# Two one-hot operands change places, gathered rows begin 14 steps later, and the query weights' low parts alternate between two engines

## The chip, the cores and the metric

One core of a Trainium2 chip runs the kernel. The metric is the device time of the program in microseconds, as the median of the runs. A second number, the span, is the time from the first to the last instruction of one profiled execution.

## The reference, cut to what matters

The reference is one encoder layer for 512 tokens of width 2048: a projection, gated linear attention and windowed attention, an output projection, and then a channel mixer with 128 x 128 = 16384 one-neuron experts. Each token has 8 heads; a head picks 16 experts by two lists of 128 keys. So a token has 128 slots, each with an expert (i, j) and a gate. The change lies in the mixer:

```python
qry = (xt @ w_query).reshape(T, PEER_HEADS, 2, PEER_QDIM // 2)
sc = jnp.einsum('thcd,hckd->thck', qry.astype(f32), sub_keys.astype(f32))
top_s, top_i = lax.top_k(sc, PEER_TOPK)
...
best_s, best_pos = lax.top_k(cand_s, PEER_TOPK)
idx = jnp.take_along_axis(cand_i, best_pos, axis=-1)
gates = jax.nn.softmax(best_s, axis=-1)
...
    u = expert_down[ib]
    act = jax.nn.gelu(jnp.einsum('tkd,td->tk', u, xb).astype(f32))
    vv = expert_up[ib]
    return jnp.einsum('tk,tkd->td', (gb * act).astype(vv.dtype), vv)
```

## The kernel before

The instructions of each engine stand in the order in which the program emits them; each engine takes its own in that order. Float32 products with weights are made as three fp32r matmuls (`mm3`): the high part of both operands, high by low, and low by high. A weight tensor comes through the class `Stream`: `load` fetches it, ScalarE casts the high part (`high`, L71), and `low` (L79) subtracts it from the raw weights on the engine that `add` was given, VectorE where nothing is said. `next` hands out a piece and prepares the one after it.

Three stages matter here.

**The query stage** (L972 on, 900 to 1170 us) runs over 8 heads. A head needs four weight pieces of 128x1024 (`wl4x` is a low part), eight (a, c) pairs of matmuls each. Between the pieces it emits the top-k work of the heads before: `pieces` runs `side` and `pairs` on VectorE, and `decode`, whose one-hot sums `oh` (L876 to L882) run on GpSimd. The four low parts of a head are made on GpSimd, VectorE, GpSimd and GpSimd.

**The gate stage** (L1127 on, 1186 to 1456 us) has 88 steps of four tokens. 352 of the 512 tokens are "dense": their activations are made for all experts and weighted by a 128 x 128 gate matrix. The matrix of one token is a product over its 128 slots: the one-hot of j (stationary) by the one-hot of i times the gate (moving). `one_hots` makes both, two steps ahead: the comparison `e` and the weighting `w` on VectorE, the copy `wj` on ScalarE, which also turns it so that the 128 keys of one token are contiguous. `w` keeps the four tokens innermost, so `w[0][:, :, u]` takes every fourth float. ScalarE copies the result to `gs`, and every eighth step stores it to `gt_d`. In between stand 246 `filler` pieces, three fp32r matmuls of 352 columns each, of the dense down product.

**The dense stage** (L1294 on, from 1472 us) has 16 rounds of 8 x 128 experts. A round's last 16 pieces multiply by the up weights (`wl2x`), 24 matmuls each; before them, from the third round on, come two half pieces for each down product. In the first two rounds the activations made before (`pre`) are weighted by the gates and split into `ah` and `al` by the class `Weighted`, partly read back from `pre_d`. After each piece `after` counts a step, and from that count starts the gathered rows: the other 160 tokens get their experts' rows by indirect DMA on GpSimd's queue (`fetch_rows`, two ahead, L1179), 1 MB each, and one VectorE instruction of 2048 columns for each row (L1193 for the down rows, L1208 for the up rows). `END` is 322, the number of rows and closing pieces, and there are 472 steps.

Of the kernel before, what the change touches and what calls it, by code (L numbers as in the profile page):

```python
# [16 lines left out]
OP = mybir.AluOpType  # L17
# [13 lines left out]
NK = 128  # L31
# [4 lines left out]
class Stream:  # L36
# [53 lines left out]
    def next(self, ahead=None):  # L90
        n = self.at
        self.halve(n + 1 + min(self.ahead if ahead is None else ahead, n))
        self.at += 1
        r = self.split[n]
        self.split[n] = None
        return r
# [3 lines left out]
def layer(ctx, tc, A, out_t, out_g, out_b):  # L100
    nc = tc.nc
    ctx.enter_context(tc.manual_schedule())

    def pool(stack, name, bufs=1, **kw):
        if kw.get("space") is not DRAM:
            kw["reuse_waits"] = "tile"
        return stack.enter_context(tc.tile_pool(name=name, bufs=bufs, **kw))

    def copy(out, in_, scale=None):
        if scale is None:  # L110
            nc.scalar.copy(out, in_)
        else:
            nc.scalar.activation(out, in_, AF.Copy, scale=scale)
# [69 lines left out]
    ws = Stream(nc, wp, "w", 2, 3, 1)  # L183
# [10 lines left out]
            ws.add(A["wout"][k, :, a:a + 4, :])  # L194
    for k in range(8):
        for a in range(0, NT, 8):
            ws.add(A["wq"][k, :, a:a + 8, :], 2, (nc.gpsimd, nc.gpsimd if a else None))

    ps = pool(front, "ps", space=PSUM)

    def pj():
        return ps.tile([128, 512], F32, name="pj", tag="pj", bufs=5)

    def pa():
        return ps.tile([128, 512], F32, name="pa", tag="pa", bufs=3)
# [4 lines left out]
    with ExitStack() as st:  # L210
# [6 lines left out]
        with ExitStack() as s2:  # L217
            ld = pool(s2, "ld", side="right")
            xt = []
            for q in range(8):  # L220
                t = ld.tile([128, 2, S], F32, name=f"xt{q}")
                for a in range(0, 2, 2 if q else 1):
                    w = 2 if q else 1
# [24 lines left out]
            for q in range(8):  # L248
                if q:
                    x_split(q, (0, 1))  # L250
                for a in range(2):
# [4 lines left out]
                    dt, k = 2 * q + a, a if q else 0  # L256
# [8 lines left out]
            for dt in range(NT):  # L265
                mm3(o_gd[:48, :], wh[:, dt, :], wl[:, dt, :], xh[:, dt, :], xl[:, dt, :], dt == 0, dt == NT - 1)
                if dt == 3:
                    b = pa()
                    for t in range(NB):
                        nc.tensor.matmul(b[:, t:t + 1], sq[:, t * 128:(t + 1) * 128], ones[:, 0:1],  # L270
                                         start=True, stop=True)
# [20 lines left out]
        with ExitStack() as s2:  # L292
# [22 lines left out]
            gd = gl.tile([48, S], F32, name="gd")  # L315
# [163 lines left out]
        with ExitStack() as s2:  # L479
# [134 lines left out]
            for g in range(3):  # L614
                e = clock[0] - 1
# [117 lines left out]
    gd = sp.tile([128, DENSE], F32, name="gd")  # L733
# [8 lines left out]
    E = 8  # L742
    EARLY, INSIDE = 3, 15
    PRE = EARLY + INSIDE + 2
# [13 lines left out]
    with ExitStack() as st:  # L758
# [133 lines left out]
        def pieces(n):  # L892
            for _ in range(min(n, len(todo))):
                todo.pop(0)()
# [10 lines left out]
        def flush():  # L905
            if late:
                late.pop().finish()
# [64 lines left out]
        for h in range(8):  # L972
            o = [pj() if h else pa() for _ in range(2)]
            for q in range(4):
                w = ws.next()
# [58 lines left out]
        def pre_store():  # L1034
            e = len(pre)
            kept = e < E
            t = prep.tile([128, DENSE], F32, name=f"pre{e}" if kept else "spill", bufs=1 if kept else 2)
            nc.vector.tensor_tensor(t, banks.pop(0), rb2[:, :DENSE], op=OP.mult)
            if not kept:
                nc.scalar.dma_start(pre_d[e], t)  # L1040
            pre.append(t)
# [8 lines left out]
        def turned_part(sel, first, n):  # L1050
            b = pa()
            for k in range(128 // n):
                rows = slice(n * k, n * k + n)
                for c in range(3):
                    nc.tensor.matmul(b[rows, c * n:(c + 1) * n], sel[rows, c, :], ident[rows, rows], start=True, stop=True)
            copy(ij[:, :, first:first + n], b[:, :2 * n].rearrange("p (c t) -> p c t", t=n))
            copy(gd[:, first:first + n], b[:, 2 * n:3 * n])

        def acts(n, *a):
            for _ in range(n):  # L1060
                yield from pre_act(*a)
# [24 lines left out]
    with ExitStack() as st:  # L1086
        gp = pool(st, "gp")
        io4 = gp.tile([128, 128, 4], BF16, name="io4")
        for k in range(4):
            if k == 0:  # L1090
                nc.gpsimd.tensor_copy(qs, ident[:, 0:NB2])
            else:
                nc.gpsimd.tensor_tensor(qs, qs, ident[:, NB2 * k:NB2 * k + NB2], op=OP.add)
        nc.vector.tensor_copy(io4, io.unsqueeze(2).to_broadcast([128, 128, 4]))

        def fill():
            yield from tail
            yield from acts(INSIDE, pa, True)

        filler, given, inside = fill(), 0, 16 * (EARLY + INSIDE) - HEAD  # L1100

        def gathered_slots():

            for b, sel in enumerate((sel_a, sel_b)):
                nc.vector.scalar_tensor_tensor(ga[b], sel[:, 0, :], 128.0, sel[:, 1, :], op0=OP.mult, op1=OP.add)
                nc.vector.tensor_copy(idx[b], ga[b])
                nc.scalar.copy(gate[b], sel[:, 2, :])

        es = {}
        STEPS = DENSE // 4  # L1110

        def one_hots(n):

            if n >= STEPS:
                return
            ts = slice(4 * n, 4 * n + 4)
            e = gp.tile([128, 2, 128, 4], BF16, name="e", bufs=3)
            nc.vector.tensor_tensor(e, ij[:, :, ts].unsqueeze(2).to_broadcast([128, 2, 128, 4]),
                                    io4.unsqueeze(1).to_broadcast([128, 2, 128, 4]), op=OP.is_equal)
            w = gp.tile([128, 128, 4], F32, name="w", bufs=3), gp.tile([128, 4, 128], F32, name="wj", bufs=3)  # L1120
            nc.vector.tensor_tensor(w[0], e[:, 0], gd[:, ts].unsqueeze(1).to_broadcast([128, 128, 4]), op=OP.mult)
            nc.scalar.copy(w[1], e[:, 1].rearrange("p k t -> p t k"))
            es[n] = w

        for k in range(2):
            one_hots(k)
        for n in range(STEPS):  # L1127
            if n % 8 == 0:
                gs = gp.tile([128, 128, 32], F32, name="gs", bufs=2)
            one_hots(n + 2)  # L1130
            if n % 4 == 1 and n < 64:
                pieces(1)
            if n in (20, 36, 52, 68):
                flush()
            if n == 38:
                turned_part(sel_h, 256, 64)
            if n == 40:
                turned_part(sel_q, 320, 32)
            while given < (n + 8) * inside // (STEPS + 8):
                next(filler)  # L1140
                given += 1
            w = es.pop(n)
            b = pj().rearrange("p (t i) -> p t i", i=128)
            for u in range(4):
                nc.tensor.matmul(b[:, u, :], w[1][:, u, :], w[0][:, :, u], start=True, stop=True)  # L1145
            copy(gs[:, :, n % 8 * 4:n % 8 * 4 + 4], b.rearrange("p t i -> p i t"))
            if n % 8 == 7:
                nc.scalar.dma_start(gt_d[n // 8].rearrange("j a x -> j (a x)"), gs.rearrange("p i t -> p (i t)"))
            if n == 70:
                gathered_slots()  # L1150
            if banks and (given + HEAD) % 16 >= 5:
                pre_store()
        for _ in filler:
            pass
        assert not todo and not late
# [26 lines left out]
    def weights_of_slots():  # L1182

        for b in range(2):
            nc.scalar.activation(ga[b], ga[b], AF.Gelu_apprx_tanh, scale=rg[:, b:b + 1])
            nc.vector.tensor_tensor(ga[b], ga[b], gate[b], op=OP.mult)
# [56 lines left out]

    pipe = []
    steps, gathered = [0], [0]
    total = 32 * (NK // E) - 2 * PRE - 12
    END = len(events)
    wait_slots = [0]

    def advance():  # L1250
        for w in pipe:
            w.step()
        while pipe and pipe[0].done == 3:
            pipe.pop(0)

    def after():

        advance()
        steps[0] += 1
        if wait_slots[0]:  # L1260
            wait_slots[0] -= 1
            if wait_slots[0] == 0:
                weights_of_slots()
            return
        while gathered[0] < min(END, steps[0] * END // total):
            gather(gathered[0])
            gathered[0] += 1
            if gathered[0] == TURN:
                wait_slots[0] = 2
                return  # L1270
# [23 lines left out]
    for sb in range(NK // E):  # L1294
        for e in range(len(av), sb * E + E):
            bank = pa()[:, :DENSE]
            for q in range(2):
                act_half(bank, q)
                after()
            av.append(Weighted(e, bank=bank))  # L1300
            pipe.append(av[-1])
        for dc in range(4):
# [8 lines left out]
            for q in range(4):  # L1311
                hi, lo = ws.next()
                for c in range(4):
                    cs = slice(c * 128, (c + 1) * 128)
                    for b in range(2):
                        w = av[sb * E + 2 * q + b]
# [86 lines left out]
```

## Time and profile before

| what | us |
|---|---|
| runs | 3346.09, 3346.30, 3348.21 |
| median | 3346.3 |
| the profiled execution | 3346.58 |
| its span | 3344.7 |
| TensorE busy | 3291.1 (98%) |
| VectorE busy | 2361.9 (71%) |
| ScalarE busy | 1183.0 (35%) |
| GpSimd busy | 917.5 (27%) |

PE is TensorE's matmuls, PEld its weight loads, DVE VectorE, ACT ScalarE, POOL GpSimd, SP the queue for plain DMAs. Matmuls overlap in the records: the distance from one start to the next tells their cost, not the length of one. An fp32 matmul leaves two records, an fp32r matmul one. Every time below is counted from the start of the span.

### The profile page before, as it was taken

To read this page: it belongs to the slowest core of one execution; us is meant where nothing else is said; L and a number is where in the kernel's file an instruction comes from. 1 tells how busy PE (TensorE), PEld (TensorE's weight loads), DVE (VectorE), ACT (ScalarE), POOL (GpSimd) and SP (SyncE) were. 2 spreads that over 40 slices of the span, in tenths; PEclk is the share of its full clock that TensorE was granted. 3 is DMA by queue.
4 is the path that set the end of the run, shared out by engine and by line. 5 is a ranking of instruction groups with operands and counts; after the bars stand their busy time and mean duration, and the time that the engine had idled before them with its cause. 6 is when DMAs were issued, how large, how long until landed. Compare 5 with 4: busy or idle time off the path is not lost.

```text
span 3344.7 us, 47641 instructions
## 1 busy us (share of the span) xinstructions
PE 3291.1 (98%) x19090; PEld 3085.0 (92%) x19090; DVE 2361.9 (71%) x3754; ACT 1183.0 (35%) x1892; POOL 917.5 (27%) x714
## 2 busy tenths in 40 slices
PE   8999999999999999998999999999999999999999
PEld 6777888888889999998999999999999999999999
DVE  5545444454456678757888888888888888888885
ACT  4334444443322245442332332332332332333332
POOL 3112020201235544322232232322232332232330
PEclk9999999999999999999999999999999999999999
DMA  4222222224322233468989898898988888988885
GB/s 148 89 91 88 76 77 84 92 101 143 117 84 72 78 126 149 156 252 337 336 327 339 324 347 331 333 350 322 338 323 327 329 338 336 334 335 330 330 347 206
DMA packets 156078, 772.94 MB, mean 231 GB/s; under 512 B 13136, under 2 KB 63632, under 8 KB 69520
## 3 DMA queue, kind: packets, MB, share of 16 engines
q1 hardware_dynamic: 99168, 388.59, 33.2%
q0 software_dynamic: 48768, 348.73, 26.4%
q10 hardware_dynamic: 7920, 32.57, 2.5%
q8 instruction: 150, 2.46, 0.3%
q14 instruction: 72, 0.59, 0.1%
HBM read 733.07 MB, written 36.77 MB: 230 GB/s over the span
## 4 chain that ended last, share of the span: by engine, by line
PE 88%; DVE 5%; DMA 2%; POOL 2%; ACT 2%; issue 1%; SPq 0%; ACTq 0%; POOLq 0%; DVEq 0%
PE pj L122 17%; PE pj L120 17%; PE pj L121 17%; PE pa L122 9%; PE pa L120 9%; PE pa L121 9%; PE pj L1145 5%; PE pa L603 1%; PE pa L544 1%; DVE wl2x L79 1%; DMA wr4x<-in_upT_dram 1%; PE pa L564 1%; DVE row L1193 1%; ACT wh2x L71 1%; POOL oh L880 0%
## 5 line engine op out<-in xcount | busy, mean ns | idle before, releaser
L79 DVE TENSOR_TENSOR wl2x<-wr4x,wh2x 128x1024 fp32r<-128x1024 f32 x382 | 467.9, 1232 | 338.7 <-ACT wh2x L71 336.0
L120 PE MATMUL pj<-ah,wh2x 128*128 128x352 f32 x2048 | 663.6, 324 | 9.3 <-ACT wh2x L71 8.9
L122 PE MATMUL pj<-ah,wl2x 128*128 128x352 f32 x2048 | 666.3, 325 | 6.3 <-DVE wl2x L79 6.3
L120 PE MATMUL pa<-yh,wh8x 128*128 128x352 f32 x2000 | 668.9, 334 | 0.0
L121 PE MATMUL pj<-al,wh2x 128*128 128x352 f32 x2048 | 661.7, 323 | 1.3 <-DVE al L1242 1.2
L122 PE MATMUL pa<-yh,wl8x 128*128 128x352 f32 x2000 | 651.5, 326 | 2.5 <-DVE wl8x L79 1.4
L121 PE MATMUL pa<-yl,wh8x 128*128 128x352 f32 x2000 | 645.3, 323 | 0.0
L71 ACT CAST wh2x<-wr4x 128x1024 fp32r<-128x1024 f32 x382 | 397.6, 1048 | 678.4 <-DMA wr4x<-in_upT_dram 337.1
L1179 POOL DMA_INDIRECT row<-in_up_dram,idx x160 | 275.8, 1724 | 610.7 <-DVE xn L1208 466.4
L1179 POOL DMA_INDIRECT row<-in_down_dram,idx x160 | 261.0, 1631 | 647.4 <-DVE ga L1193 639.5
L122 PEld LDWEIGHTS pj<-ah,wl2x 128*128 128x128 f32 x2048 | 386.5, 189 | 13.0 <-DVE wl2x L79 10.3
L120 PEld LDWEIGHTS pj<-ah,wh2x 128*128 128x128 f32 x2048 | 386.3, 189 | 12.1 <-ACT wh2x L71 10.5
L121 PEld LDWEIGHTS pj<-al,wh2x 128*128 128x128 f32 x2048 | 387.5, 189 | 2.3 <-DVE al L1242 2.1
L120 PEld LDWEIGHTS pa<-yh,wh8x 128*128 128x128 f32 x2000 | 377.5, 189 | 1.7
L121 PEld LDWEIGHTS pa<-yl,wh8x 128*128 128x128 f32 x2000 | 377.3, 189 | 1.6
L122 PEld LDWEIGHTS pa<-yh,wl8x 128*128 128x128 f32 x2000 | 374.2, 187 | 4.0 <-DVE wl8x L79 1.9
L79 DVE TENSOR_TENSOR wl8x<-wr16x,wh8x 128x1024 fp32r<-128x1024 f32 x220 | 268.3, 1222 | 106.6 <-ACT wh8x L71 106.3
L71 ACT CAST wh8x<-wr16x 128x1024 fp32r<-128x1024 f32 x256 | 266.8, 1046 | 183.5 <-DMA wr16x<-in_downT_dram 123.4
L1208 DVE SCALAR_TENSOR_TENSOR xn<-row,ga,xn 128x2048 f32<-128x2048 f32 x127 | 297.9, 2345 | 0.0
L1193 DVE CUSTOM_DVE_ANT_0 row<-row,xn 128x2048 f32<-128x2048 f32 x128 | 292.4, 2284 | 0.0
L120 PE MATMUL pj<-wh2x,xh 128*128 128x512 f32 x704 | 284.7, 404 | 0.0
L121 PE MATMUL pj<-wl2x,xh 128*128 128x512 f32 x704 | 275.4, 391 | 1.2 <-DVE wl2x L79 1.2
(330 smaller groups left out, 4959.7 us busy)
## 6 DMA issues: line engine op xcount, KB each, us to landing
wr16x<-in_downT_dram SPq DMA_DIRECT2D x128, 1024.0 KB, 7.1
wr4x<-in_upT_dram SPq DMA_DIRECT2D x128, 1024.0 KB, 7.1
wr4x<-in_win_dram SPq DMA_DIRECT2D x47, 1024.0 KB, 4.9
gt_d<-gs ACTq DMA_DIRECT2D x11, 2048.0 KB, 6.5
g<-gt_d SPq DMA_DIRECT2D x30, 704.0 KB, 8.5
wr4x<-in_wout_dram SPq DMA_DIRECT2D x16, 1024.0 KB, 5.0
wr8x<-in_wq_dram SPq DMA_DIRECT2D x16, 1024.0 KB, 5.0
xt<-in_xT_dram POOLq DMA_DIRECT2D x4, 1024.0 KB, 6.5
```

The lines of the kernel that those rows point to most:

```text
L71: self.nc.scalar.copy(hi, t)
L79: self.lo_engine[n].tensor_tensor(lo, t, hi.bitcast(F32), op=OP.subtract)
L120: nc.tensor.matmul(out, sh, mh, start=first, stop=False)
L121: nc.tensor.matmul(out, sh, ml, start=False, stop=False)
L122: nc.tensor.matmul(out, sl, mh, start=False, stop=last)
L544: nc.tensor.matmul(sc[u], qt[:, h, t * 128:(t + 1) * 128], kt[:, h, :], start=True, stop=True)
L564: nc.tensor.transpose(tp[:, kb * 128:(kb + 1) * 128], prs[u][:, kb * 128:(kb + 1) * 128], ident)
L603: nc.tensor.matmul(oo, vv[:, kb, h * 128:(h + 1) * 128], pt[u][:, kb, :], start=kb == 0, stop=kb == NB - 1)
L1145: nc.tensor.matmul(b[:, u, :], w[1][:, u, :], w[0][:, :, u], start=True, stop=True)
L1179: nc.gpsimd.indirect_dma_start(out=t, out_offset=None, in_=A["up" if up else "down"], in_offset=bass.IndirectOffsetOnAxis(ap=idx[b][:, k:k ...
L1193: nc.vector.tensor_tensor_reduce(t, t, x, 1.0, 0.0, OP.mult, OP.add, g[:, k:k + 1])
L1208: nc.vector.scalar_tensor_tensor(x, t, g[:, k:k + 1], x, op0=OP.mult, op1=OP.add)
```

## The change

Three edits. First, `add` for the query weights gives GpSimd the first piece of each load and VectorE the second. Second, in the gate stage the gate is multiplied onto the one-hot of j, which becomes the stationary operand and is read in steps of four floats; the plain one-hot of i is turned by ScalarE and streamed contiguously. The product is the same. Third, no row is started in the first 14 steps, and the count of steps over which the rows are spread is 448 and no longer 460.

```diff
-            ws.add(A["wq"][k, :, a:a + 8, :], 2, (nc.gpsimd, nc.gpsimd if a else None))
+            ws.add(A["wq"][k, :, a:a + 8, :], 2, (nc.gpsimd,))
...
-            nc.vector.tensor_tensor(w[0], e[:, 0], gd[:, ts].unsqueeze(1).to_broadcast([128, 128, 4]), op=OP.mult)
-            nc.scalar.copy(w[1], e[:, 1].rearrange("p k t -> p t k"))
+            nc.vector.tensor_tensor(w[0], e[:, 1], gd[:, ts].unsqueeze(1).to_broadcast([128, 128, 4]), op=OP.mult)
+            nc.scalar.copy(w[1], e[:, 0].rearrange("p k t -> p t k"))
...
-                nc.tensor.matmul(b[:, u, :], w[1][:, u, :], w[0][:, :, u], start=True, stop=True)
+                nc.tensor.matmul(b[:, u, :], w[0][:, :, u], w[1][:, u, :], start=True, stop=True)
...
-    total = 32 * (NK // E) - 2 * PRE - 12
+    total = 32 * (NK // E) - 2 * PRE - 24
...
-        while gathered[0] < min(END, steps[0] * END // total):
+        while gathered[0] < min(END, max(0, steps[0] - 14) * END // total):
```

On GpSimd, in the query stage, this is the end of the top-k chain of one head and the low parts behind it:

```order
 L880 TENSOR_TENSOR oh<-oh 128x128
 L882 TENSOR_TENSOR sel_d<-oh 128x2x2x16
-L79 TENSOR_TENSOR wl4x_7509<-wr8x_7176,wh4x_7507 128x1024
 L79 TENSOR_TENSOR wl4x_7576<-wr8x_7301,wh4x_7574 128x1024
 L79 TENSOR_TENSOR wl4x_7737<-wr8x_7511,wh4x_7735 128x1024
```

The low part of the head's fourth piece leaves the place behind `sel_d`. On VectorE it comes in at this place of the same head, behind the comparison `eqa`:

```order
 L869 TENSOR_SCALAR smk<-bv 128x1 x2
 L873 TENSOR_TENSOR eqa<-pf,io_7039 128x1024
+L79 TENSOR_TENSOR wl4x_7509<-wr8x_7176,wh4x_7507 128x1024
 L784 TENSOR_TENSOR xb<-pa,g2b 128x512
 L928 TENSOR_TENSOR qT<-pj,rb_6105 128x512 x2
```

It is the same in the other heads. On VectorE at the start of the dense stage, where the last of the first eight `al` is made and the first two groups of the first round end, there stood before (ISA is the row instruction and the read of its sum):

```order
L1236 TENSOR_TENSOR pre_10975<-pre_10975,g 128x352
L1193 ISA row,ga_9855<-row,xb 128x2048
L1193 ISA ga_9855 128x1
L79 TENSOR_TENSOR wl2x_12738<-wr4x_12563,wh2x_12736 128x1024
L1242 TENSOR_TENSOR al<-pre_10975,ah 128x352
L1193 ISA row,ga_9855<-row,xb 128x2048
L1193 ISA ga_9855 128x1
L79 TENSOR_TENSOR wl2x_12773<-wr4x_12646,wh2x_12771 128x1024
L1321 TENSOR_TENSOR x_12484<-x_12484,pj 128x352 x4
```

The same place now:

```order
L1236 TENSOR_TENSOR pre_10975<-pre_10975,g 128x352
L79 TENSOR_TENSOR wl2x_12735<-wr4x_12563,wh2x_12733 128x1024
L1242 TENSOR_TENSOR al<-pre_10975,ah 128x352
L79 TENSOR_TENSOR wl2x_12767<-wr4x_12646,wh2x_12765 128x1024
L1321 TENSOR_TENSOR x_12484<-x_12484,pj 128x352 x4
```

The rows between the low parts are gone here; the first one now stands at the sixteenth step, at the end of the first round.

## Rows read from the trace of the kernel before

**Rows 1.** The chain that ended last: shares of the span by engine.
```profile
PE 88%; DVE 5%; DMA 2%; POOL 2%; ACT 2%; issue 1%; SPq 0%; ACTq 0%; POOLq 0%; DVEq 0%
```
**Rows 2.** Stretches: us, busy PE, PEld, DVE, ACT, POOL; PEclk, DMA share, GB/s.
```profile
900.00:1170.00 270.00, 255.21 (x1796) 246.92 (x1796) 154.13 (x775) 73.30 (x163) 126.67 (x98) 0.97 0.23 77
...
1186.00:1390.00 204.00, 204.00 (x1077) 193.12 (x1076) 174.82 (x385) 102.56 (x179) 82.87 (x46) 1.00 0.38 144
1390.00:1456.00 66.00, 66.00 (x341) 62.72 (x340) 36.25 (x50) 31.16 (x52) 11.99 (x5) 1.00 0.40 148
...
1456.00:1540.00 84.00, 73.97 (x424) 70.63 (x423) 52.21 (x65) 25.88 (x37) 19.04 (x13) 0.94 0.88 333
1540.00:1640.00 100.00, 93.63 (x565) 90.23 (x565) 85.30 (x105) 34.85 (x49) 28.60 (x17) 1.00 0.91 335
...
1640.00:2340.00 700.00, 700.00 (x4320) 698.96 (x4319) 591.65 (x656) 221.45 (x265) 203.69 (x125) 1.00 0.89 335
```
**Rows 3.** Waits, 900 to 1190 us: who for whom, us, times, longest.
```profile
PE pj L122 <- POOL wl4x L79: 14.6, 6, 3.0
...
PEld pj L122 <- POOL wl4x L79: 16.4, 6, 3.3
```
**Rows 4.** Timeline around the first such wait: start, length, instruction, [idle before <-releaser].
```profile
934.29 0.69 DVE L873 TENSOR_TENSOR eqa<-pf,io 128x1024 bf16<-128x1024 bf16 x1
...
939.79 0.69 DVE L784 TENSOR_TENSOR xb<-pa,g2b 128x512 f32<-128x512 f32 x1 [4.82 <-ACT xr L783]
...
934.95 1.03 ACT L71 CAST wh4x<-wr8x 128x1024 fp32r<-128x1024 f32 x1
...
939.70 0.30 POOL L882 TENSOR_TENSOR sel_d<-oh 128x64 f32<-128x64 bf16 x1
...
939.96 4.70 POOL L79 TENSOR_TENSOR wl4x<-wr8x,wh4x 128x1024 fp32r<-128x1024 f32 x2
...
942.38 0.43 PE L122 MATMUL pj<-yh,wl4x 128*128 128x352 f32 x1 [2.90 <-POOL wl4x L79]
```
**Rows 5.** Groups of instructions of VectorE: low parts, row instructions.
```profile
L79 DVE TENSOR_TENSOR wl8x<-wr16x,wh8x 128x1024 fp32r<-128x1024 f32 x220 | 268.3, 1222 | 106.6 <-ACT wh8x L71 106.3
...
L1193 DVE CUSTOM_DVE_ANT_0 row<-row,xn 128x2048 f32<-128x2048 f32 x128 | 292.4, 2284 | 0.0
```
**Rows 6.** Busy time by stretch, right after two of the waits.
```profile
942.00:947.00 5.00, 4.62 (x23) 4.63 (x23) 0.00 (x0) 0.15 (x1) 2.66 (x2) 0.66 0.73 231
...
1012.00:1018.00 6.00, 5.35 (x21) 5.35 (x22) 0.00 (x0) 0.37 (x1) 2.92 (x2) 0.50 0.53 175
```
**Rows 7.** Chain and timeline: start, length, records of fp32 matmuls and of weight loads.
```profile
1314.88 0.16 PE pa L121
...
1316.18 1.81 PE pj L1145 x8
...
370.30 1.79 PE pa L603 x16
...
899.55 0.97 PEld L795 LDWEIGHTS pa<-ones,sq 128*128 128x128 f32 x8
```
**Rows 8.** Instructions of tile e, VectorE: ns minimum/median/maximum.
```profile
L1118 DVE TENSOR_TENSOR e<-ij,io x88: 669/685/2883, 1174.6 to 1445.4; 128x1024 bf16<-128x1024 bf16 x88
L1121 DVE TENSOR_TENSOR w<-e,gd x88: 691/693/2880, 1176.4 to 1446.1; 128x512 f32<-128x512 bf16 x88
```
**Rows 9.** The first rounds of the dense stage: waits, chain, and stretches.
```profile
PE pj L120 <- ACT wh2x L71: 7.9, 3, 6.0
PE pj L122 <- DVE wl2x L79: 5.4, 8, 1.3
...
1503.64 11.88 DMA wr4x<-in_upT_dram
...
1506.00:1520.00 14.00, 7.65 (x38) 6.91 (x38) 3.30 (x6) 3.04 (x3) 0.00 (x0) 0.76 0.85 350
...
1550.00:1560.00 10.00, 6.68 (x37) 5.52 (x36) 9.86 (x16) 3.75 (x7) 3.22 (x2) 1.00 0.76 259
```

## The prediction

> **What bounds the kernel now.** I read the chain of waits first. It runs through TensorE for 88% of the span [rows 1]. So work on another engine counts only where TensorE waits for it, and a change in TensorE's own instructions counts in full, until another engine becomes later. Next I read the busy time by stretch, and it names three places [rows 2]. In the query stage (900 to 1170 us) TensorE is busy 255.21 of 270 us, at a mean granted clock of 0.97. In the gate stage (1186 to 1456 us) it is never idle. In the first two rounds of the dense stage (1456 to 1640 us) it is idle 10.0 + 6.4 us. From 1640 to 2340 us it is busy without a gap although VectorE is busy 591.65 of 700 us. The diff has one edit for each of the three places.
>
> **Part 1, the low parts of the query weights.** In each of the 8 rounds over the heads, one of the three 128x1024 subtractions on GpSimd moves to VectorE. The waits tell why it matters: TensorE's matmuls wait for GpSimd's `wl4x` six times, 14.6 us in all, and the weight loads 16.4 us [rows 3]. One of them in full: the high part is ready at 934.95 + 1.03 = 935.98 us, but GpSimd first finishes the `oh` chain of the top-k, whose last piece is the `sel_d` at 939.70 us, and starts `wl4x` at 939.96; the matmul at 942.38 us has waited 2.90 us. VectorE, behind its `eqa` at 934.29 us, is idle 4.82 us until 939.79 [rows 4]. In the new order the subtraction stands exactly there, between `eqa` and `xb`. At 1.22 us (the mean of VectorE's `wl8x` row of the same size [rows 5]) it would be done near 937.2 us, before TensorE asks at about 939.3. On GpSimd the next round's `wl4x` moves up by 2.4 us; TensorE needs that one a whole granule later.
>
> A wait costs more than its length. [...] The first stretch loses (1 - 0.66) x 5 = 1.7 us, the third (1 - 0.50) x 6 less what of it lies in the wait itself, 2.7 us. Four of the six waits are near 3 us and are followed by this (3 x 1.7 + 2.7 = 7.8 us); after the two of 1.4 us the clock stays at 1.0.
> The sum: 16.4 (wait up to the weight load) + 7.8 = 24.2 us; I take 24. Lower bound: the two short waits stand where VectorE is itself busy with the top-k, and some others could be only shortened: 15. Upper bound 25. The 8 x 1.22 = 10 us added to VectorE cost nothing: it is busy 154.13 of 270 us there [rows 2]. But VectorE runs in order, so the top-k pieces behind the moved subtraction wait with it for the high part; what waits for those is GpSimd's `oh` and, much later, the selections. That is slack of several us each round.
>
> **Part 2, the one-hots change roles.** A step makes four fp32 128x128 matmuls, two records each. In the gate stage eight records take 1.81 us, 0.226 each; where the moving operand is contiguous (L603, same shape and type) sixteen take 1.79 us, 0.112 each [rows 7]. The moving operand `w` is read here in steps of four floats, so the step doubles the streaming. A weight load of 128 contiguous columns costs 0.111 us: eight loads whose matmuls have a single column take 0.97 us, which is seven distances and one last load of 0.192 [rows 7]. At L603 load and stream therefore tie at 0.11 and overlap; at L1145 the stream of 0.226 hides the load. The swap gives the stream 0.112. It gives the load the step of four floats, and no row of the trace has a load with a step. Bounds:
> - The load is as fast as a contiguous one: a step takes 8 x 0.112 = 0.90 instead of 1.81 us, 88 x 0.91 = 80 us less on TensorE.
> - The load doubles as the stream does, to 0.222, still under the matmul before it: 0.06 (the first load against a 0.16 us matmul) + 7 x 0.222 + 0.112 = 1.73 us, 88 x 0.08 = 7 us less.
> - The load doubles and does not overlap: 8 x (0.222 + 0.112) = 2.67 us, 88 x 0.86 = 76 us more.
> I take the second, since the nearest row is the same tile read with the same step by the same engine. [...]
>
> In the first case VectorE caps the gain. From 1186 to 1390 us (66 steps) it is busy 174.82 of 204 us [rows 2], and TensorE would want only 204 - 66 x 0.91 = 144; so at most 29 us can go there. From 1390 to 1456 (22 steps) VectorE needs 36.25 us only, and 20 us go in full: 49 us. Less if VectorE's stretched instructions (`e` has a median of 0.685 and a maximum of 2.883 us, `w` 0.693 and 2.880 [rows 8]) are those that meet GpSimd's work: 66 x 1.38 = 91 us of them unstretched + 82.87 us of GpSimd + some 20 us of top-k that doesn't fall under it = 194 us; then 10 + 20 = 30 us. I take 40.
>
> **Part 3, the rows begin 14 steps later.** Before, 16 x 322 // 460 = 11 gathered rows are worked off in the 16 steps of the first round; now 2 x 322 // 448 = 1. That takes 10 x 2.28 us [rows 5] of VectorE and 10 MB of row loads out of the round in which the queue is fullest. The largest wait there is 6.0 us [rows 9]: the up weights issued at 1503.64 us land after 11.88 us, with the DMA engines 0.85 busy. TensorE is busy 7.65 of 14 us in that stretch, at a granted clock of 0.76: 6.3 us idle, and of the (1 - 0.76) x 14 = 3.4 us about half while it works, together 8.0. Eight waits for VectorE's low parts, `wl2x`, make another 5.4 us, the longest 1.3 us. They come thickest from 1550 to 1560 us: there TensorE is idle 3.3 us, with VectorE busy 9.86 of 10 us [rows 9]. A low part that stands behind a row of 2.28 us loses up to that; with the rows gone I count 4 of the 5.4 us, since the waits after 1560 us lie in the round that keeps its rows. So 12 us are in reach. Other loads stay (the stored activations, x1, gates), and the new first rows still meet the last `pre` and `al` pieces: I take 10. On the other side the rows run at 322/448 = 0.719 a step for 0.700; that is 0.019 x 2.3 = 0.04 us in a step of 3.9 us, 1.1% on a VectorE that is 85% busy without stopping TensorE [rows 2]. Priced at 0, up to 5 us if it makes new waits. The last row falls on step 462 of 472, ten steps (39 us) before the end, so the tail is unmoved. Net 10, from 12 gained to 3 lost.
>
> **The sum.** 24 + 7 + 10 = 41 us off the profiled execution's 3346.6 us (span 3344.7, median 3346.3, so the same within 0.01%): **3306 us**, own range 3297 to 3324.
>
> **The rivals.**
> - *The load with a step costs nothing.* For it: a load takes 0.111 us for 128 columns where the fp32r stream takes 0.16 for 352 [rows 7], so loading is the slower reader and may have time to spare for each element. Against: the fp32 stream reads at that same pace and was slowed. It gives 24 + 40 + 10 = 74: 3273 us (3256 to 3290), with VectorE the bound of the gate stage. [...]
> - *The load with a step holds up the stream (slower).* Place: L1145, 704 records. If such a load isn't hidden under the matmul before it, the record is 0.334 instead of 0.226 us: 76 - 34 = 42 us more, 3389 us. It turns slower above a record of 0.226 + 34/704 = 0.274 us. Against: in all other rows loads are hidden.
> - *The waits come back elsewhere.* VectorE, late with the top-k, delays the moved subtractions, and the denser rows give back what the first round gains: only part 2's 7 us stay, 3340 us, at the edge of what can be told from no change (0.2% is 7 us, about the measurement's limit). Against: VectorE's idle 4.82 us at the very place.
>
> **How the numbers follow.** Chances: forecast 0.50, free load 0.36, held-up stream 0.07, waits come back 0.07. The time is the forecast's, 3306. The range takes the forecast's own range and the free load's: 3255 to 3324. Both are faster by over 0.2%: 0.86; same 0.07; slower 0.07.
>
> **What would show it.** In the changed profile: no TensorE wait for GpSimd's `wl4x`, and a granted clock of 1.0 in the query stage, 24 us shorter. Eight L1145 records in about 1.73 us (forecast), 0.90 with gaps that end on VectorE's `w` (free load), 2.67 (held up); weight loads of L1145 recorded near 0.30 us instead of 0.19 would mean the doubled load. No row before the sixteenth step, the 6.0 us wait gone. The forecast is wrong if the gate stage changes by more than 10 us either way.

## The result and the profile after

| kernel | runs | median, us (lowest to highest) | ratio, 95% interval |
|---|---|---|---|
| before | 4 | 3347.26 (3346.09 to 3350.04) | 1 |
| after | 4 | 3316.95 (3313.98 to 3324.67) | 0.9912 [0.9893, 0.9931] |

The change takes 30 us off, 0.9%. 3306 was forecast, 41 us off. The profiled execution of after took 3315.02 us, with a span of 3312.9. TensorE's share of the chain of waits is 89%, GpSimd's 0% where it was 2% [rows 1]:

```profile
PE 89%; DVE 5%; DMA 3%; ACT 2%; issue 1%; POOL 0%; ACTq 0%; DVEq 0%; POOLq 0%
```

**The query stage.** Busy time by stretch in after: TensorE is busy 267.22 of 270 us at a granted clock of 1.00, where it was 255.21 at 0.97 [rows 2]. The two stretches behind the old waits, 0.66 and 0.50 [rows 6], are at 1.00:

```profile
900.00:1170.00 270.00, 267.22 (x1909) 259.54 (x1910) 173.65 (x811) 82.25 (x178) 128.25 (x101) 1.00 0.27 89
...
942.00:947.00 5.00, 5.00 (x39) 5.00 (x38) 2.49 (x3) 0.00 (x0) 1.18 (x1) 1.00 0.20 76
1012.00:1018.00 6.00, 6.00 (x46) 5.55 (x46) 1.83 (x10) 2.95 (x5) 0.28 (x1) 1.00 0.28 107
```

All of TensorE's waits in after from 900 to 1190 us (for whom, us, times, longest). Those for GpSimd's `wl4x` [rows 3] are gone, none has come in their place (the two for `wl8x` stood there before with the same numbers):

```profile
PE pj L122 <- POOL wl8x L79: 1.3, 1, 1.3
PE pa L122 <- POOL wl8x L79: 1.1, 1, 1.1
PE pa L178 <- DVE dg L177: 0.2, 1, 0.2
```

The timeline of after at the place of [rows 4], VectorE and then GpSimd (start, length, instruction, idle before):

```profile
933.79 0.69 DVE L873 TENSOR_TENSOR eqa<-pf,io 128x1024 bf16<-128x1024 bf16 x1
935.50 2.21 DVE L79 TENSOR_TENSOR wl4x<-wr8x,wh4x 128x1024 fp32r<-128x1024 f32 x1 [1.03 <-ACT wh4x L71]
939.30 0.69 DVE L784 TENSOR_TENSOR xb<-pa,g2b 128x512 f32<-128x512 f32 x1 [1.58 <-ACT xr L783]
...
934.62 2.02 POOL L876 TENSOR_TENSOR oh<-eqa,tf 128x1024 bf16<-128x1024 bf16 x1 [4.16 <-DVE eqa L873]
936.71 3.27 POOL L880 TENSOR_TENSOR oh<-oh 128x512 bf16<-128x512 bf16 x3
```

The subtraction stands where the order put it, in what was VectorE's idle time; 1.03 us before it and 1.58 behind it are left of the 4.82. It takes 2.21 us here, beside GpSimd's `oh`, not 1.22.

**The gate stage.** Line L1145 in after (ns minimum/median/maximum, first to last start), the chain, and two stretches:

```profile
L1145 PEld LDWEIGHTS pj<-wj,w x704: 308/329/332, 1162.7 to 1432.3; 128*128 128x128 f32 x176
L1145 PE MATMUL pj<-wj,w x704: 338/397/398, 1162.9 to 1432.5; 128*128 128x128 f32 x176
```
```profile
1290.15 1.81 PE pj L1145 x8
```
```profile
1163.00:1367.00 204.00, 204.00 (x1075) 203.65 (x1074) 174.21 (x385) 102.73 (x179) 82.02 (x46) 1.00 0.38 142
1367.00:1433.00 66.00, 66.00 (x339) 66.00 (x339) 36.51 (x50) 31.10 (x53) 11.94 (x5) 1.00 0.39 146
```

The stage begins 23 us earlier (the first L1145 stood at 1185.9 us in before) and is as long as before: 269.6 us from the first to the last record, 268.9 before. Eight records take 1.81 us as in [rows 7]. What has changed is the weight loads: they are busy 203.65 of 204 us where they were 193.12, and 66.00 of 66 where they were 62.72 [rows 2].

**The dense stage.** TensorE's waits in after from 1433 to 1640 us, to be held against [rows 9]:

```profile
PE pj L122 <- DVE wl2x L79: 2.7, 4, 0.8
PE pj L120 <- ACT wh2x L71: 1.6, 1, 1.6
PE pj L121 <- DVE al L1242: 1.6, 2, 1.2
PE pj L120 <- ACT ah L1238: 0.8, 2, 0.4
PE pa L122 <- DVE wl8x L79: 0.5, 1, 0.5
```

The 6.0 us wait for `wh2x` is gone (7.9 us in three became 1.6 in one), and 5.4 us for `wl2x` became 2.7. From the last L1145 to the end of the span the kernel takes 1880.4 us, where it took 1889.9: 9.5 less. So 23.0 - 0.7 + 9.5 = 31.8 us, the difference of the two spans (3344.7 and 3312.9), stand against the 24 + 7 + 10 of the forecast. The last of these is read from one execution of each kernel; over all the profiled executions it is 1880 to 1888 us there with the third edit, and 1890 to 1891 without it where all rows are loaded.

### The profile page after: what moved, and what is told of

Read it like the earlier page. It is cut to its first block, busy times and chain, and to the rows that moved or that the text cites. A ratio compares the mean times of both kernels' runs of the same rounds, so it can differ in the third digit from the quotient of the medians.

```text
span 3312.9 us, 47648 instructions
## 1 busy us (share of the span) xinstructions
PE 3279.6 (99%) x19090; PEld 3088.2 (93%) x19090; DVE 2369.9 (72%) x3762; ACT 1181.1 (36%) x1892; POOL 906.6 (27%) x706
## 4 chain that ended last, share of the span: by engine, by line
PE 89%; DVE 5%; DMA 3%; ACT 2%; issue 1%; POOL 0%; ACTq 0%; DVEq 0%; POOLq 0%
PE pj L122 17%; PE pj L120 17%; PE pj L121 17%; PE pa L120 9%; PE pa L122 9%; PE pa L121 9%; PE pj L1145 5%; PE pa L603 1%; PE pa L544 1%; DMA wr4x<-in_upT_dram 1%; DVE wl2x L79 1%; DVE row L1193 1%; DMA wr16x<-in_downT_dram 1%; PE pa L932 1%; PE pa L564 1%
## 5 line engine op out<-in xcount | busy, mean ns | idle before, releaser
L120 PE MATMUL pj<-ah,wh2x 128*128 128x352 f32 x2048 | 662.9, 324 | 2.4 <-ACT wh2x L71 1.6
L121 PE MATMUL pj<-al,wh2x 128*128 128x352 f32 x2048 | 661.4, 323 | 1.8 <-DVE al L1242 1.6
L120 PE MATMUL pa<-yh,wh8x 128*128 128x352 f32 x2000 | 659.7, 330 | 0.7 <-ACT wh8x L71 0.7
L121 PE MATMUL pa<-yl,wh8x 128*128 128x352 f32 x2000 | 645.0, 322 | 0.0
L121 PEld LDWEIGHTS pj<-al,wh2x 128*128 128x128 f32 x2048 | 387.2, 189 | 3.2 <-DVE al L1242 2.9
L120 PEld LDWEIGHTS pj<-ah,wh2x 128*128 128x128 f32 x2048 | 385.8, 188 | 3.8 <-ACT wh2x L71 2.3
L120 PEld LDWEIGHTS pa<-yh,wh8x 128*128 128x128 f32 x2000 | 378.5, 189 | 1.9 <-ACT wh8x L71 1.0
L121 PEld LDWEIGHTS pa<-yl,wh8x 128*128 128x128 f32 x2000 | 376.0, 188 | 0.0
L120 PE MATMUL pj<-wh2x,xh 128*128 128x512 f32 x704 | 284.9, 405 | 0.0
L121 PE MATMUL pj<-wl2x,xh 128*128 128x512 f32 x704 | 275.1, 391 | 1.2 <-DVE wl2x L79 1.2
```

The costliest lines, as they stand in the source:

```text
L120: nc.tensor.matmul(out, sh, mh, start=first, stop=False)
L121: nc.tensor.matmul(out, sh, ml, start=False, stop=False)
```

## The experiments

All times below stand beside runs of the kernel before on the same chip: 3349.45 us for the first four, 3349.87 for e5 to e8, 3350.99 for e9 to e11, 3350.4 for e12.

### The three parts apart

Part 1 alone, on the kernel before:

```diff
-            ws.add(A["wq"][k, :, a:a + 8, :], 2, (nc.gpsimd, nc.gpsimd if a else None))
+            ws.add(A["wq"][k, :, a:a + 8, :], 2, (nc.gpsimd,))
```


> The kernel before with the first part alone: the query weights' low parts alternate between GpSimd and VectorE. Theory (three separate parts: the waits for GpSimd's low parts and the lower clock after them are worth 23 us, the one-hots nothing, the rows 9 to 10): 3347 - 23 = 3324 us, first L1145 record near 1163 us, none of the six waits for wl4x, granted clock 1.0 in the query stage. Rival (the gain of the whole came mostly from later stages, since the query stage only hands its time on to the wait for the gates at 1456 us): under 10 us, so 3337 us or more.

3326.20 us (3321.73 to 3328.85), ratio 0.9932 [0.9915, 0.9948]: 23 us less. TensorE is busy 267.21 of 270 us in the query stage, as in after.

Part 2 alone:

```diff
-            nc.vector.tensor_tensor(w[0], e[:, 0], gd[:, ts]...
-            nc.scalar.copy(w[1], e[:, 1].rearrange("p k t -> p t k"))
+            nc.vector.tensor_tensor(w[0], e[:, 1], gd[:, ts]...
+            nc.scalar.copy(w[1], e[:, 0].rearrange("p k t -> p t k"))
...
-                nc.tensor.matmul(b[:, u, :], w[1][:, u, :], w[0][:, :, u], start=True, stop=True)
+                nc.tensor.matmul(b[:, u, :], w[0][:, :, u], w[1][:, u, :], start=True, stop=True)
```


> The kernel before with the second part alone: the one-hots change places. Theory (a load of weights in steps of four floats takes as long as the stream in such steps did, and is the longer of two that overlap): eight L1145 records in 1.81 us as before, load records near 0.33 us, 3347 us, within 2. My prediction's term: 7 us less, 3340. Rival (the swap is worth something that the other parts hide): 3335 or less.

3350.27 us (3346.80 to 3353.46, 10 runs), ratio 1.0002 [0.9992, 1.0012]. The exchange does nothing to the time, within 4 us either way. By the traces it costs a little: the gate stage is 269.6 us long here and in after, and 268.9 us in each of the six kernels with the roles and steps of before.

Part 3 alone:

```diff
-    total = 32 * (NK // E) - 2 * PRE - 12
+    total = 32 * (NK // E) - 2 * PRE - 24
...
-        while gathered[0] < min(END, steps[0] * END // total):
+        while gathered[0] < min(END, max(0, steps[0] - 14) * END // total):
```


> The kernel before with the third part alone: rows from the fourteenth step on, spread over 448 steps. Theory: the 6.0 us wait for the up weights and two thirds of the waits for wl2x go, about 3 us come back in later rounds: 3347 - 9 = 3338 us. Rival (rows only moved: what the first round gains, the denser rest loses): 3347 us, within 3.

3343.11 us (3336.55 to 3345.80, 10 runs), ratio 0.9980 [0.9971, 0.9990]: 6.3 us less, between 3 and 10, where 9 were expected.

The changed kernel with part 2 undone (the reverse of the second diff):

> The changed kernel with the one-hots put back. Theory: the same as the changed kernel, 3316 us, within 2. Rival (the swap costs or brings some us beside the two other parts): differs from the changed kernel's 3317 by more than 4 us.

3318.32 us (3317.36 to 3321.77), ratio 0.9913 [0.9897, 0.9930]: the time of after. So the result is the sum of parts 1 and 3; on the same chip the third part takes 7.9 us off the kernel with the first part alone.

### Why the exchange of roles gives nothing

Three kernels tell whether the step of four floats is at fault, what a step of two costs, and what two operands with the step of four cost together. In the first, VectorE writes the weighted one-hot with the tokens outside, so both operands are read contiguously (the diff is against after):

```diff
-            w = gp.tile([128, 128, 4], F32, name="w", bufs=3), gp.tile([128, 4, 128], F32, name="wj", bufs=3)
-            nc.vector.tensor_tensor(w[0], e[:, 1], gd[:, ts].unsqueeze(1).to_broadcast([128, 128, 4]), op=OP.mult)
+            w = gp.tile([128, 4, 128], F32, name="w", bufs=3), gp.tile([128, 4, 128], F32, name="wj", bufs=3)
+            nc.vector.tensor_tensor(w[0], e[:, 1].rearrange("p k t -> p t k"), gd[:, ts].unsqueeze(2).to_broadcast([128, 4, 128]), op=OP.mult)
...
-                nc.tensor.matmul(b[:, u, :], w[0][:, :, u], w[1][:, u, :], start=True, stop=True)
+                nc.tensor.matmul(b[:, u, :], w[0][:, u, :], w[1][:, u, :], start=True, stop=True)
```


> The changed kernel, but VectorE writes the weighted one-hot with the tokens outermost, so that both operands of the gate matmuls are read contiguously. Theory (whichever operand has the step of four floats sets the 0.226 us of a record): the record falls to about 0.112 us, 88 x 0.91 = 80 us leave TensorE's own work in the gate stage, VectorE then bounds it, and 30 to 49 us are left: about 3277 us (3265 to 3290), with gaps of TensorE that end on VectorE. Rival (the record's length has to do with the fp32 one-hots or with their two operands being new each time, not with the step): records stay at 0.226 us and the time at 3317. Second rival (VectorE writes slower with a step on its 16-bit reads): the weighting of 0.69 us takes about 1.2 us, 88 x 0.5 = 44 us more of VectorE, and the gain is gone: 3310 to 3330.

3273.24 us (3269.68 to 3281.02), ratio 0.9770 [0.9749, 0.9792]: 44 us under after by the medians. After ran on another chip; by the ratios to before it is 47. Line L1145 of this kernel, its chain late in the stage, two stretches (columns as before: PE, PEld, DVE, ACT, POOL, PEclk, DMA, GB/s) and the largest wait from 1160 to 1420 us:

```profile
L1145 PEld LDWEIGHTS pj<-wj,w x704: 186/192/338, 1164.0 to 1388.1; 128*128 128x128 f32 x176
L1145 PE MATMUL pj<-wj,w x704: 270/275/553, 1164.2 to 1388.2; 128*128 128x128 f32 x176
```
```profile
1366.08 0.89 PE pj L1145 x8
```
```profile
1160.00:1360.00 200.00, 175.64 (x1219) 169.46 (x1218) 186.58 (x407) 111.27 (x201) 93.74 (x50) 0.96 0.44 165
1360.00:1390.00 30.00, 30.00 (x223) 30.00 (x222) 24.73 (x28) 19.67 (x33) 7.98 (x3) 1.00 0.54 196
```
```profile
PE pj L1145 <- DVE w L1121: 22.8, 15, 2.5
```

The load's record is back from 0.329 to 0.192 us, and eight records take 0.89 us, not 1.81: 88 x 0.92 = 81 us less for TensorE. The stage shrinks from 269.6 to 224.0 us, by 45.6: VectorE is now busy 186.58 of 200 us, and TensorE, idle 24 of them, waits for its `w`. Writing `w` in the other order costs VectorE nothing: its median stays at 0.693 us. The second rival falls by that.

In the second kernel `w` keeps two tokens innermost (against after):

```diff
+            w = gp.tile([128, 2, 128, 2], F32, name="w", bufs=3), gp.tile([128, 4, 128], F32, name="wj", bufs=3)
...
+                nc.tensor.matmul(b[:, u, :], w[0][:, u // 2, :, u % 2], w[1][:, u, :], start=True, stop=True)
```


> The changed kernel, but the weighted one-hot keeps only two tokens innermost, so that the stationary operand is read in steps of two floats (8 bytes), not four. [...] Rival (any step costs the same): the record stays at 0.226 us, 3317 us. [...]

3275.29 us (3272.05 to 3282.80), ratio 0.9779 [0.9758, 0.9799]. Its chain:

```profile
1366.07 0.93 PE pj L1145 x8
```

A step of two floats costs 0.04 us in eight records, a step of four 0.92. No run has a step of three or of eight floats, so where between two and four the cost begins, and how it goes on, is not shown.

In the third kernel both operands have the step of four (against after):

```diff
-            nc.scalar.copy(w[1], e[:, 0].rearrange("p k t -> p t k"))
+            nc.scalar.copy(w[1], e[:, 0])
...
-                nc.tensor.matmul(b[:, u, :], w[0][:, :, u], w[1][:, u, :], start=True, stop=True)
+                nc.tensor.matmul(b[:, u, :], w[0][:, :, u], w[1][:, :, u], start=True, stop=True)
```


> The changed kernel, but ScalarE copies the other one-hot without turning it, so that both operands are read in steps of four floats. Theory (a stepped load is hidden under the matmul before it, and each of the two reads at its own half rate): eight records take 1.81 us as with one of them stepped, 3317 us. Rival (the two reads share one path and add): 0.45 us a record, 88 x 1.8 = 160 us more, 3475 us.

3327.74 us in one run. Its chain:

```profile
1200.94 1.92 PE pj L1145 x8
```

1.92 us, not the 3.6 of 1.81 twice: a slow load and a slow stream go on beside each other, and 88 x 0.11 = 10 us are what they cost together beyond one of them. The stage is 279.2 us long here, 9.6 more than in after. So the two reads don't add, and the rival by which a stepped load holds up the stream is out.

Last, the roles of before with both operands contiguous (against the first of these kernels):

```diff
-            nc.vector.tensor_tensor(w[0], e[:, 1].rearrange("p k t -> p t k"), gd[:, ts]...
-            nc.scalar.copy(w[1], e[:, 0].rearrange("p k t -> p t k"))
+            nc.vector.tensor_tensor(w[0], e[:, 0].rearrange("p k t -> p t k"), gd[:, ts]...
+            nc.scalar.copy(w[1], e[:, 1].rearrange("p k t -> p t k"))
...
-                nc.tensor.matmul(b[:, u, :], w[0][:, u, :], w[1][:, u, :], start=True, stop=True)
+                nc.tensor.matmul(b[:, u, :], w[1][:, u, :], w[0][:, u, :], start=True, stop=True)
```


> The changed kernel with the one-hots in the roles of before (the gate on the moving operand), but both written so that they are read contiguously. Theory (the step alone costs, on whichever side it stands; the exchange of roles is worth nothing by itself): the time is that of the kernel with contiguous operands and exchanged roles, 3273 us within 5 us, the record 0.11 us. Rival (the exchange is needed for the gain): the record stays near 0.2 us, 3300 to 3317 us.

3273.42 us (3272.32 to 3277.61), ratio 0.9769 [0.9754, 0.9783]: the same as with the roles exchanged. It is the step that costs, on whichever side it stands: the median of L1145's matmul records is 0.275 us in both roles when both operands are contiguous, 0.405 with the step on the moving operand (before) and 0.397 with it on the stationary one (after).

### What the later rows gain by

The kernel before, without the loads of rows 3 to 8:

```diff
-    fetched = {}
+    fetched, held = {}, {}
...
+            if 3 <= n < 9:
+                fetched[n] = held[(0, 1, 0, 1, 1, 2)[n - 3]]
+                return
...
+            if n < 3:
+                held[n] = t
```


> The kernel before, with the loads of the gathered rows 3 to 8 left out (VectorE's work on them stays, on row tiles held from rows 0 to 2; the sums of these rows are not the reference's). It asks whether the 6 to 10 us of the later rows come from the queue or from VectorE. Queue theory: 6 MB less in the first round of the dense stage, the wait of 6.0 us for the up weights goes, and 6 to 8 us are gained, about 3341 us. VectorE theory: the instructions of 2.28 us stand where they stood, so the time stays within 2 us of before, 3348 us, and the waits for wl2x stay at 5 us.

3341.40 us (3337.59 to 3342.62, 9 runs), ratio 0.9972 [0.9962, 0.9983]: 8.5 us less. Its waits from 1430 to 1640 us, and the stretch in which TensorE was busy 7.65 of 14 us at a clock of 0.76 [rows 9]:

```profile
PE pj L122 <- DVE wl2x L79: 4.7, 6, 1.3
PE pj L120 <- ACT wh2x L71: 1.8, 2, 1.6
```
```profile
1506.00:1520.00 14.00, 14.00 (x88) 13.94 (x88) 10.59 (x13) 4.21 (x4) 1.32 (x1) 1.00 0.56 191
```

VectorE does all its row instructions here, and the waits for its `wl2x` stay near the old 5.4 us. The 6.0 us wait is gone with 6 MB of loads. GpSimd issues six loads fewer as well, but what ended the wait in before was the landing of a load [rows 9]. So it was the loads, as the prediction had it, and the waits for VectorE are the smaller share.

The kernel before with the denser rows but without the delay:

```diff
-    total = 32 * (NK // E) - 2 * PRE - 12
+    total = 32 * (NK // E) - 2 * PRE - 24
```


> The kernel before with the rows spread over 448 steps, not 460, but begun at once, without the 14 steps of delay: what the denser rows cost by themselves. Forecast's bounds: 0 to 5 us slower, 3349 to 3354 us. Theory of the small later losses (VectorE, 1.1% more row work per step, lets TensorE wait a few us in the later rounds): 2 to 4 us slower. Rival (they cost nothing): within 1 us. Below nothing is possible only if the earlier end of the rows frees the last steps: 1 us.

3347.97 us (3346.85 to 3351.84, 11 runs), ratio 0.9993 [0.9984, 1.0002]: between 5 us less and 1 us more. The denser rows cost nothing that can be measured; whether they gain a little stays open.

### What bounds the gate stage when the step is gone

The timeline of the kernel with contiguous operands (start, length, instruction):

```profile
1251.29 0.69 DVE L1121 TENSOR_TENSOR w<-e,gd 128x512 f32<-128x512 bf16 x1
1251.31 2.90 POOL L79 TENSOR_TENSOR wl8x<-wr16x,wh8x 128x1024 fp32r<-128x1024 f32 x1
...
1251.90 2.87 DVE L1118 TENSOR_TENSOR e<-ij,io 128x1024 bf16<-128x1024 bf16 x1
```

GpSimd's subtraction ends at 1254.21 us, 2.31 us after the start of `e`, and `e`, 0.69 us by itself, ends 0.56 us after that: it seems to wait for GpSimd nearly from its start. It is no single case: of the 88 comparisons of this kernel 26 take over 1 us, and each of them ends 0.55 or 0.56 us after an instruction of GpSimd, 22 after such a subtraction and 4 after an `oh` of the top-k. In after it is the same: 15 of the 88 take over 1 us, and each ends 0.54 to 0.56 us after an instruction of GpSimd, 11 after such a subtraction and 4 after an `oh`. The test puts 26 of these low parts on VectorE (against the kernel with contiguous operands):

```diff
-        ws.add(A["downT"][e], 2, () if e >= EARLY + INSIDE else (nc.gpsimd, nc.gpsimd))
+        ws.add(A["downT"][e], 2, () if e >= EARLY + 2 else (nc.gpsimd, nc.gpsimd))
```


> The changed kernel with both operands contiguous, and 26 low parts of the filler pieces of the gate stage made on VectorE, not on GpSimd. Theory (VectorE bounds the stage there because its comparisons and weightings, 0.69 us alone, are stretched by GpSimd's low parts): 26 x 1.22 = 32 us are added to VectorE and 37 to 45 us of stretching go, so it is 5 to 13 us less busy, TensorE's 22.8 us of waits for w shrink by as much: 3260 to 3268 us, the mean of e near 0.75 us. Rival (the stretching is not from the low parts): e stays at 1.17 us in the mean, VectorE gets 32 us more, 3295 to 3305 us.

3262.71 us (3261.91 to 3267.88), ratio 0.9743 [0.9728, 0.9758]: the fastest of all, 54 us under after by the medians, 57 by the ratios. VectorE's groups from 1160 to 1390 us (count, busy us, mean ns), first with the low parts on GpSimd, then here:

```profile
L1118 DVE TENSOR_TENSOR e<-ij,io 128x1024 bf16<-128x1024 bf16 x84 | 98.6, 1174 | 0.0
```
```profile
L1118 DVE TENSOR_TENSOR e<-ij,io 128x1024 bf16<-128x1024 bf16 x84 | 60.5, 720 | 0.0
L79 DVE TENSOR_TENSOR wl8x<-wr16x,wh8x 128x1024 fp32r<-128x1024 f32 x29 | 37.6, 1298 | 8.8 <-ACT wh8x L71 8.8
```

The comparisons fall from 98.6 to 60.5 us, by 38; the subtractions bring 35 (37.6 less the 2.4 that stood on VectorE already). So the stretching came from the subtractions. With `w` and the pieces of the top-k, which are stretched less too, VectorE is busy 200.6 us from 1160 to 1390, where it was 211.3:

```profile
1160.00:1360.00 200.00, 178.39 (x1287) 172.59 (x1286) 183.29 (x440) 117.51 (x211) 38.26 (x27) 0.99 0.47 175
1360.00:1390.00 30.00, 30.00 (x209) 30.00 (x209) 17.27 (x24) 15.14 (x25) 0.25 (x1) 1.00 0.59 229
```

TensorE's waits for `w` fell less than expected, from 22.8 to 18.7 us. The last kernel asks whether these are bursts (against the one just shown):

```diff
-            w = gp.tile([128, 4, 128], F32, name="w", bufs=3), gp.tile([128, 4, 128], F32, name="wj", bufs=3)
+            w = gp.tile([128, 4, 128], F32, name="w", bufs=4), gp.tile([128, 4, 128], F32, name="wj", bufs=4)
...
-        for k in range(2):
+        for k in range(3):
...
-            one_hots(n + 2)
+            one_hots(n + 3)
```


> The kernel with both operands contiguous and the 26 low parts on VectorE, with the one-hots made three steps ahead and four buffers for each operand, where there were two steps and three buffers. What is left there are 18.7 us of TensorE waiting for w, with VectorE busy 92% from 1160 to 1360 us. Theory (the rest is partly bursts: VectorE stands 6.2 us for a free buffer before the first step and is then late behind the top-k): 2 to 6 us less, 3257 to 3261 us, the waits for w 12 to 16 us. Rival (VectorE's throughput alone is the bound): the waits stay at 18 us and the time at 3263 within 2 us.

3265.47 us (3265.16 to 3266.59), ratio 0.9746 [0.9729, 0.9762]. The wait for `w` from 900 to 1640 us:

```profile
PE pj L1145 <- DVE w L1121: 13.3, 15, 2.0
```

The waits fell into the theory's 12 to 16 us and the stage from 214.9 to 213.0 us, but the whole got no faster, and the forecast of 3257 to 3261 was missed: by the medians it is 3 us slower, so some 5 us were lost outside the gate stage. In the profiled executions they lie behind it: from the last L1145 to the end of the span it is 1888.0 us, where the kernel just shown took 1881.1. The instructions there are the same, and the kernel with the roles of before has 1888.4 in its execution, so this may be scatter. Why the part behind the stage varies so is not settled, and the intervals of the two kernels overlap.

## Why the prediction was right, and where it was not

The time, 3316.95, lies 11 us above the forecast and inside its own range of 3297 to 3324. By the spans 31.8 us came of 41; nearly 8 of the 9 missing are part 2.

**Part 1: 24 forecast, 23 measured.** Alone it is 23 us as well. Both pieces of the sum are there, the waits and the clock behind them (granted 0.66 in 5 us and 0.50 in 6 us [rows 6], both now 1.00). The same work, from 860 us to the first L1145, in before and in after:

```profile
860.00:1185.90 325.90, 308.70 (x2095) 295.24 (x2094) 175.10 (x803) 90.55 (x195) 150.66 (x116) 0.97 0.25 83
```
```profile
860.00:1162.90 302.90, 300.12 (x2093) 287.93 (x2091) 183.60 (x811) 90.20 (x194) 137.87 (x108) 1.00 0.27 89
```

TensorE's idle time falls from 17.2 to 2.8 us, by 14.4, and its busy time by 8.6. So the 16.4 us of the weight loads' waits were 2 too many, since matmuls still run while the next load waits; the 14.6 us of the matmuls' own waits [rows 3] were the better figure, and 7.8 for the clock was a little short. The lower bound wasn't needed: the two short waits went too. The moved subtraction was sized wrongly, 2.21 us for 1.22: its price was that of a row away from GpSimd. It cost nothing because 4.82 us were idle there. Over all of `wl4x` on VectorE the price is between the two:

```profile
L79 DVE TENSOR_TENSOR wl4x<-wr8x,wh4x x16: 1212/1564/2211, 881.7 to 1115.0; 128x1024 fp32r<-128x1024 f32 x16
```

The median of the sixteen in after is 1.56 us (minimum/median/maximum in ns). Together they take 24.4 us, where the eight of before took 10.6; so the eight that are new cost some 14 us of VectorE, not 10, and as little on the path.

**Part 2: 7 forecast, 0 measured.** The mechanism that was chosen is the right one. The load doubles (0.231 us from one to the next, where contiguous ones have 0.11 [rows 7] to 0.12), its record goes from 0.208 to 0.329 us, and it becomes the longer of the two. The step that failed is the size of one term, the 0.222 us for a stepped load. The forecast set its sum of 1.73 us against the 1.81 of the chain, and the chain counts from the end of one record to the end of the next. Counted so, the last seven of a step's eight records, and the matmul behind them, are these, first in before, then in after:

```profile
1316.40 1.59 PE pj L1145 x7
1317.99 0.16 PE pa L120
```
```profile
1290.33 1.64 PE pj L1145 x7
1291.97 0.17 PE pa L120
```

In after each takes 1.64/7 = 0.234 us, where the forecast had 0.222; in before it is 1.59/7 = 0.227. The first record takes 1.81 - 1.64 = 0.17 us, as the forecast had it (0.06 + 0.112). So 7 x 0.012 = 0.08 us a step were missing, and 88 x 0.08 = 7 us are the whole term: beside the stepped stream that it replaced, the stepped load is a little slower and not a little faster. No row of before has a load with a step, as the prediction says, and twice the contiguous distance was the guess.

The starts of the records tell the same in another way. TensorE's records around the same steps, first before, then after:

```profile
1316.02 1.97 PE L1145 MATMUL pj<-w,wj 128*128 128x128 f32 x8
1317.63 0.52 PE L120 MATMUL pa<-yh,wh8x 128*128 128x352 f32 x1
1317.99 0.32 PE L121 MATMUL pa<-yl,wh8x 128*128 128x352 f32 x1
```
```profile
1289.99 1.98 PE L1145 MATMUL pj<-wj,w 128*128 128x128 f32 x8
1291.72 0.41 PE L120 MATMUL pa<-yh,wh8x 128*128 128x352 f32 x1
1291.97 0.32 PE L121 MATMUL pa<-yl,wh8x 128*128 128x352 f32 x1
```

From the first L1145 to L121 it is 1.97 us in before and 1.98 in after, no difference. From the first L1145 to L120 it is 1.73 us in after, the very number of the forecast, but counted so before has 1.61 and not 1.81: the agreement is chance. L120 begins before the group is done and only seems long by its start (0.36 and 0.25 us until L121).

The weight loads of after and of the kernel with both operands contiguous:

```profile
1289.83 1.95 PEld L1145 LDWEIGHTS pj<-wj,w 128*128 128x128 f32 x8
```
```profile
1368.11 1.02 PEld L1145 LDWEIGHTS pj<-wj,w 128*128 128x128 f32 x8
```

The distance of the loads is (1.95 - 0.33)/7 = 0.231 us in after, and (1.02 - 0.19)/7 = 0.12 with both operands contiguous.

**Part 3: 10 forecast, 9.5 in the whole, 6.3 alone** with an interval of 3 to 10, and 7.9 beside part 1. The largest wait and its 14 us stretch went as the prediction priced them (8.0), and the runs show the loads as their cause (8.5 with 6 MB not loaded). The waits for `wl2x` fell by 2.7 us; 4 were counted. The bound of 5 us for the denser rows was too wide: 1 us at most. There is a little new idle time later in after:

```profile
1617.00:2310.00 693.00, 690.47 (x4261) 687.84 (x4261) 590.55 (x653) 217.58 (x262) 207.68 (x128) 1.00 0.89 339
```

2.5 us are idle here, where the kernel before had none from 1640 to 2340 us. The later rows by themselves don't make it: from 1640 to 2340 us TensorE has no gap with part 3 alone or with the denser rows, and 1.0 us with parts 1 and 3 together. It may be the other meeting points of rows and pieces when the stage begins earlier; that is not shown.

**The rivals.** The *free load* needed a load that the step doesn't slow; the load's record shows the opposite (0.329 us for 0.208). Its numbers were right where the load really is fast: the kernel with both operands contiguous has the 0.89 us for 0.90, VectorE as the bound, and 45.6 us for the 40 that were taken between 30 and 49. With the same 128 columns the distance of two loads is 0.11 [rows 7] to 0.12 us contiguous and 0.231 with a step of four floats. *Held-up stream* and *waits come back* did not happen. The gate stage changed by 0.7 us, within the 10 that the prediction allowed.

## What to carry to other kernels

Ask of each operand of a matmul in what step it is read: with a step of four floats it was read at half the rate, as stationary operand and as moving one (eight records in 1.81 us, 0.89 with both contiguous), with a step of two, as stationary operand, at nearly the full one (0.93), and exchanging the two operands only moves the cost. Writing the operand contiguously in the instruction that makes it anyway cost VectorE nothing here (0.693 us either way) and was worth 44 us. A sum of parts and the number that it is set against must be counted alike, from start to start or from end to end. A load that is hidden under a stream can become the longer of the two without any wait in the profile: look at the weight loads' busy share (here 193 of 204 became 203.65) before counting a faster stream as a gain. Price an instruction that moves next to GpSimd's work at its stretched duration (here 2.21 us beside `oh`), not at its mean (1.22).

## What the runs showed of the hardware that was not expected

- The weight load with a step of four floats: 0.329 us a record for 0.192, distance 0.231 for 0.12; in the chain 0.234 a record, where the stream with that step had 0.227. With a step of two floats eight records take 0.93 us for 0.89.
- A load and a stream that both have the step of four cost 1.92 us for eight records together (one run), either alone 1.81.
- The record of the first fp32r matmul behind a group of fp32 ones begins before the group is done: 0.25 to 0.36 us from its start to the next, though 0.16 to 0.17 in the chain.
- VectorE's comparison of 0.69 us became 2.87 us where GpSimd's subtraction began 0.59 us before it: it ended 0.56 us after the subtraction; 26 subtractions moved to VectorE there cost it 26 x 1.30 = 34 us, and its comparisons alone get 38 us back.
